# First feed-forward's closing: post steps over two products and the value projection, squares in another order, four adds later

## The chip, the cores and the metric

The kernel runs on one core of a Trainium2 chip. The metric is the device time of one execution in microseconds (us); lower is better. The kernel before takes 2013.42 us, the median of three runs (2012.97 to 2015.08). The engines are named as in the profile: PE (TensorE, matrix products), DVE (VectorE), ACT (ScalarE), POOL (GpSimd) and SP (SyncE, which here issues the transfers).

## The reference

A trunk of two layers over 1024 positions of width 1024, all in float32. Layer A is a gated linear recurrence beside a memory attention; layer B is a sliding-window attention over shared keys and values beside a memory attention. Each is followed by an output projection and a feed-forward of inner width 2816. Around each mixer and each feed-forward stands a norm before and one after ("sandwich"); the one after the feed-forward is the one that the change touches:

```python
def swiglu_ffn(x, w_in, w_out):
    gu = x @ w_in
    g, u = gu[..., :D_FF], gu[..., D_FF:]
    return (jax.nn.silu(g) * u) @ w_out
...
f = swiglu_ffn(rms_norm(h, norm_ffn_pre[l]), w_ffn_in[l], w_ffn_out[l])
h = h + rms_norm(f, norm_ffn_post[l])
if l == N_A_LAYERS - 1:
    kv = rms_norm(h, norm_kv) @ w_kv_shared
```

After the first layer's feed-forward the shared keys (with a partial rotary) and values are projected from the residual; layer B reads them. The last lines of the kernel's feed-forward and the first of layer B therefore follow each other on every engine.

## The kernel before

Every float32 product is made of three matmuls of rounded halves, low by high, high by high and high by low. A tile is split into its halves by a cast on ACT (line 92; the names `th`, `ch`, `ah`, `mkh`) and a subtraction on DVE (line 93; `tl`, `cl`, `al`; `mkl` and `kl` are made by the same pair at 302 and 304). The 1024 positions are two halves of 512, and a tile is 128 x 512.

The feed-forward's output projection is a seven-product scheme. Products 1, 6, 7, 4, 2, 5, 3 run in this order; each has 11 steps of 12 matmuls (L761 to L763) whose operands are loaded and split just in time in rings of a few tiles. Four groups of four accumulators are collected: `c11` and `c21` are the first half of the positions, `c12` and `c22` the second. `c21` is last written behind product 4, `c11` behind product 2. So the first half is whole while products 5 and 3 still run, and its closing lies under these two: `squares` sums the squares of eight tiles (ACT square, DVE addition, L227), PE sums over the partitions with a product by ones (L237), DVE and POOL make the reciprocal root (L241, L242), PE spreads it over the partitions again (L249), and `ffn_post` scales each of the eight tiles (L944), adds the residual that SP has loaded (L947), stores the tile and splits it for the next stage. The second half gets its last addend behind product 3 (L865, and L898, which adds the parts of product 5 to `c22`); its closing is the function `fin`, which layer B calls from `done` in the middle of its value projection.

Layer B's `half` sums the squares of its own norm (`s`, L213), copies the spread root to `rsn` (L253), makes two query products for the memory attention (evicted with `rsn` at L411), two key products with the rotary (`rope`, L1071 to L1074: DVE evicts `kf` and a shuffled copy, POOL multiplies and adds), then four value products (L1183 to L1185, evicted to `vv` by ACT at L349 and DVE at L350), and then six query products with the rotary. Memory keys and values come with two loads (`pb` from `mkv`) and are expanded to `mkh`, `mkl` and `mvv`. PE's products of this stage share three banks named "mm"; a product waits until the one three before it has been evicted. Attention units (scores L382, L383, L1100, L1101 to `ss`, transposes to `tt`, outputs to `oo`) are put between the products by a table of quotas; the products of the later half of the positions serve as their cover.

Every engine takes its instructions in the order of one queue. That order comes from a scheduler that goes by priorities and its own estimates. `self.after(x, y)` binds it without a wait on the chip: x is placed after y in the schedule, no more. `POST_STEPS` lists the steps of products 5 and 3 (`steps[12 * i]`, the first matmul of step i) behind which the eight L944 of the first half are placed. `END_PLACES` does the same for the matmuls that follow L237 and L249. `fin` gives no steps before the change.

Of the kernel before, what the change touches and what calls it, by code (L numbers as in the profile page):

```python
# [10 lines left out]
ALU = mybir.AluOpType  # L11
# [6 lines left out]
KT = D // P  # L18
NM = 256
# [19 lines left out]
NEXT_WEIGHTS = ([("wb", NL), ("wb", NL + 1), ("wk", 0), ("wk", 1), ("wv", 0), ("wv", 1)] +  # L39
                [("wb", j) for j in range(NL)] + [("wo", m) for m in range(KT)])  # L40
OPEN_LEAD = 150
POST_STEPS = 4, 5, 7, 8, 10, 12, 13, 15
LATE_PRODUCTS = 2, 5, 3
OUT_PARTS = {1: (0, 0), 2: (1, 0), 3: (1, 0), 4: (1, 1), 5: (1, 1), 6: (0, 0), 7: (0, 1)}
NO_SYNC = mybir.DependencyInfo(mybir.DependencyClass.NoSync, mybir.DependencyReason.DATA)
# [3 lines left out]
class Trunk:  # L49
# [744 lines left out]
    def ffn(self, layer, x, act, hx, finish, dst, final):  # L794
        nc = self.nc
# [56 lines left out]
        gpost = G_FFN_POST + 8 * layer  # L852
# [19 lines left out]
        def squares(f, tags, who, own):  # L872
            tiles = [(e, self.t(tag)) for e, tag in tags]
            take = self.sums(tiles, who, own)
            for m in range(KT):
                take(m, f[m])
            return [x for _, x in tiles]

        ps, w0 = None, []
        for i, c in ((1, c11), (6, c12), (7, c22), (4, c21)):  # L880
            ps = total(i, [(c, None)], ps)
# [11 lines left out]
        if not final:  # L893
            total(3, [(c12, c12)], ps)
            steps = order[5] + order[3]
            h0 = self.ffn_post(f0, rs, 0, gpost, r0, dst, [steps[12 * i] for i in POST_STEPS])
            for x, y in zip(c22, part):
                nc.vector.tensor_tensor(x, x, y, op=ALU.add)  # L898
            for i, g in zip(END_PLACES, marks):
                self.after(steps[i], g[-1])  # L900

            def fin():
                s = self.t("s")
                for k in range(KT):
                    self.sumsq(s, f1[k], k == 0)
                rs1 = self.rstd(s, "p")[1]
                return self.ffn_post(f1, rs1, 1, gpost, lambda k: self.load(self.part(hx, k, 1), "pb"), dst)

            return (*h0, w0), fin
        self.post(f0, rs, 0, gpost, r0, dst)  # L910
# [226 lines left out]
    def layer_b(self, h0, finish):  # L1137
        nc, a = self.nc, self.a
        mask = self.t("mask", (P, 2 * P))
        nc.sync.dma_start(mask, a["mask"])  # L1140
        y = [[None] * KT for _ in range(2)]
        kk = [[None] * 2 for _ in range(4)]
        vv = [None] * 8
        self.mem_tags = 1

        def half(n, act, f, w0, done):
            acts = [act, act]
            s = self.t("s")
            take = self.sums([(nc.vector, s)], "00000000", ("sq",))
            for k in range(KT):  # L1150
                take(k, f[k])
            rc = self.rcol(s, f"n{n}")
            rs = self.spread(rc, self.t("rsn"))
            tab = []
            for name in ("cos", "sin"):
                t_ = self.t(name)
                nc.sync.dma_start(t_, a[name][:, n * H:n * H + H])
                nc.gpsimd.tensor_tensor(t_, t_, rs, op=ALU.mult)
                tab.append(t_)
            for j in range(2):  # L1160
                w = w0.pop(0) if w0 else self.fetch(("wb", NL + j))
                y[n][NL + j] = self.mem_query(w, acts, n, rs)
                done()
            for j in range(2):
                kf = self.t("kf")
                w = w0.pop(0) if w0 else self.fetch(("wk", j))
                self.rope(kf, self.proj(w, acts, n), tab)
                for e in range(2):
                    gi = 2 * j + e
                    if n == 0:  # L1170
                        kk[gi][n] = self.t(f"kh{gi}", dt=F32R), self.t(f"kl{gi}", dt=F32R)
                    else:
                        kk[gi][n] = self.act_tile()
                    self.kdup(kf, 64 * e, *kk[gi][n])
                done()
            wv = [self.fetch(("wv", j), 4) for j in range(2)]
            for i in range(4):
                ps = self.psum("mm")
                sl = slice(i * P, i * P + P)
                for k in range(KT):  # L1180
                    wh, wl = wv[k // 4]
                    ah, al = act[k]
                    nc.tensor.matmul(ps[:, :NM], al[:, sl], wh[:, k % 4], start=k == 0, stop=False)  # L1183
                    nc.tensor.matmul(ps[:, :NM], ah[:, sl], wh[:, k % 4], start=False, stop=False)
                    nc.tensor.matmul(ps[:, :NM], ah[:, sl], wl[:, k % 4], start=False, stop=k == KT - 1)  # L1185
                if n == 0:
                    v = self.t(f"vv{i}", dt=F32R)
                else:
                    if i % 2 == 0:
                        vt = self.act_tile()  # L1190
                    v = vt[i % 2]
                vv[4 * n + i] = v.rearrange("p (g c) -> p g c", g=4)
                self.vsplit(vv[4 * n + i], ps[:, :NM], rc[:, i:i + 1])
                if i % 2:
                    done()
            for j in range(NL):
                y[n][j] = self.acc_tile()
                self.rope(y[n][j], self.proj(self.fetch(("wb", j)), acts, n), tab)
                done()

        kvf = [self.load(d, "pb").rearrange("p (i c) -> p i c", i=2) for d in self.kv1]
        kv = {}

        def units(n):
            us = []

            def mem(j, e):
                if not kv:
                    kv.update({i: self.mem_expand(kvf, i) for i in range(2)})
                return self.mem_unit(y[n][NL + j], e, kv[j], y[n][NL + j])  # L1210

            for j in range(2):
                for e in range(2):
                    us.append(lambda j=j, e=e: mem(j, e))
            for h in range(2 * NL):
                us.append(lambda h=h: self.swa_unit(h, n, y[n][h // 2], kk, vv, mask))
            return us

        ready = []

        def step(n):
            us, at = units(n), [0]

            def done():
                i = at[0]
                at[0] += 1
                if n == 1 and i == PACED_FROM:
                    self.mms = []
                if n == 0 and i == 9:
                    h1.extend(finish())  # L1230
                if i == 3:
                    for j, u in enumerate(us[:4]):
                        ready.insert(MEM_UNITS[j], u)
                elif i >= 6:
                    ready.extend(us[2 * i - 8:2 * i - 6])
                for _ in range(min(QUOTA[n][i], len(ready))):
                    self.attend(ready.pop(0))

            return done

        h1 = []
        half(0, *h0, step(0))
        half(1, *h1, None, step(1))
        order = [6, 7, 0, 1, 2, 3, 4, 5]
        return self.mix_out(1, y, order, self.h1, ready, [(f"k{h}{i}",) for h in "hl" for i in range(4)])
# [68 lines left out]
```

## Time and profile before

| what | value |
|---|---|
| median of three runs | 2013.42 us |
| the profiled execution | 2016.41 us |
| its span, first to last instruction | 2014.6 us |
| PE / DVE / ACT / POOL busy | 98 / 70 / 51 / 21 % of the span |
| closing of the first feed-forward, products 5 and 3 | about 925 to 990 us |
| layer B up to the value projection's end | 990 to 1031 us |
| attention of layer B, first half | up to about 1215 us |
| second feed-forward's closing | from about 1928 us |

The profiled execution is one of its own and 3.0 us above the median; 1.8 us of it lie outside the span. In a list of instructions the columns are start, duration, engine, line, operation and tiles; the square brackets hold the idle time of the engine just before and what ended it. Several alike in a row are one line (x4), with their common duration. Buffer numbers are left out of the names in the trace and stand in the orders below. A matmul's duration includes its passage through the array; the next one starts earlier than it ends.

### The profile page before, as it was taken

To read this page: it belongs to the slowest core of one execution; us is meant where nothing else is said; L and a number is where in the kernel's file an instruction comes from. 1 tells how busy PE (TensorE), PEld (TensorE's weight loads), DVE (VectorE), ACT (ScalarE), POOL (GpSimd) and SP (SyncE) were. 2 spreads that over 40 slices of the span, in tenths; PEclk is the share of its full clock that TensorE was granted. 3 is DMA by queue.
4 is the path that set the end of the run, shared out by engine and by line. 5 is a ranking of instruction groups with operands and counts; after the bars stand their busy time and mean duration, and the time that the engine had idled before them with its cause. 6 is when DMAs were issued, how large, how long until landed. Compare 5 with 4: busy or idle time off the path is not lost.

```text
span 2014.6 us, 27759 instructions
## 1 busy us (share of the span) xinstructions
PE 1965.2 (98%) x9360; PEld 1633.8 (81%) x9360; DVE 1408.1 (70%) x2345; ACT 1019.3 (51%) x1943; POOL 419.2 (21%) x435
## 2 busy tenths in 40 slices
PE   8999999999999999999999999999999999999997
PEld 7887878888888888888788778887888888888887
DVE  7788867977766676456887888679656655654566
ACT  6678764443444444454534768545333333344551
POOL 0122100034443330000035353100233222300001
PEclk9999999999999999999999999999999999999998
DMA  5422436167668789775454123171644444586653
GB/s 177 160 84 79 152 105 240 68 210 265 227 244 274 251 289 314 236 239 168 148 194 172 65 92 128 58 276 54 204 136 167 158 151 154 194 300 192 218 181 115
DMA packets 182685, 359.60 MB, mean 178 GB/s; under 512 B 20112, under 2 KB 25488, under 8 KB 182544
## 3 DMA queue, kind: packets, MB, share of 16 engines
q1 hardware_dynamic: 182544, 357.85, 52.8%
q8 instruction: 73, 1.20, 0.2%
q14 instruction: 68, 0.56, 0.1%
HBM read 251.86 MB, written 105.91 MB: 178 GB/s over the span
## 4 chain that ended last, share of the span: by engine, by line
PE 80%; DVE 9%; ACT 5%; issue 3%; DMA 2%; POOL 1%; SPq 0%; POOLq 0%; DVEq 0%; ACTq 0%
PE mm L653 13%; PE mm L655 13%; PE mm L654 13%; PE mm L761 6%; PE mm L762 6%; PE mm L763 6%; PE mm L154 5%; PE mm L152 5%; PE mm L153 5%; PE oo L1131 1%; DVE al L93 1%; ACT pb L96 1%; PE oo L237 1%; ACT L96 1%; DVE tl L93 1%
## 5 line engine op out<-in xcount | busy, mean ns | idle before, releaser
L92 ACT CAST ch<-wq 128x512 fp32r<-128x512 f32 x311 | 193.2, 621 | 424.2 <-PE mm L654 217.8
L93 DVE TENSOR_TENSOR cl<-wq,ch 128x512 fp32r<-128x512 f32 x311 | 231.6, 745 | 192.3 <-ACT ch L92 116.2
L653 PE MATMUL mm<-al,ch 128*128 128x512 f32 x640 | 252.4, 394 | 0.0
L655 PE MATMUL mm<-ah,cl 128*128 128x512 f32 x640 | 251.0, 392 | 0.0
L654 PE MATMUL mm<-ah,ch 128*128 128x512 f32 x640 | 250.3, 391 | 0.0
L152 PE MATMUL mm<-al,wh 128*128 128x512 f32 x568 | 228.0, 401 | 9.0 <-DVE al L996 7.4
L154 PE MATMUL mm<-ah,wl 128*128 128x512 f32 x568 | 227.0, 400 | 1.0 <-DVE wl L93 1.0
L153 PE MATMUL mm<-ah,wh 128*128 128x512 f32 x568 | 225.7, 397 | 0.0
L761 PE MATMUL mm<-tl,ch 128*128 128x512 f32 x532 | 207.4, 390 | 2.1 <-DVE tl L93 2.1
L762 PE MATMUL mm<-th,ch 128*128 128x512 f32 x532 | 207.0, 389 | 0.0
L763 PE MATMUL mm<-th,cl 128*128 128x512 f32 x532 | 205.2, 389 | 0.5 <-DVE cl L93 0.5
L653 PE MATMUL mm<-tl,ch 128*128 128x512 f32 x480 | 188.8, 393 | 0.8 <-DVE tl L93 0.8
L655 PE MATMUL mm<-th,cl 128*128 128x512 f32 x480 | 188.4, 393 | 0.0
L654 PE MATMUL mm<-th,ch 128*128 128x512 f32 x480 | 187.3, 390 | 0.0
L664 DVE TENSOR_TENSOR c<-c,mm 128x512 f32<-128x512 f32 x120 | 82.3, 686 | 113.5 <-PE mm L655 113.5
L655 PEld LDWEIGHTS mm<-ah,cl 128*128 128x128 f32 x640 | 120.1, 188 | 28.1
L654 PEld LDWEIGHTS mm<-ah,ch 128*128 128x128 f32 x640 | 120.2, 188 | 26.4
L653 PEld LDWEIGHTS mm<-al,ch 128*128 128x128 f32 x640 | 120.2, 188 | 26.0
L152 PEld LDWEIGHTS mm<-al,wh 128*128 128x128 f32 x568 | 108.5, 191 | 31.6 <-DVE al L996 7.4
L154 PEld LDWEIGHTS mm<-ah,wl 128*128 128x128 f32 x568 | 108.4, 191 | 24.9 <-DVE wl L93 1.7
L153 PEld LDWEIGHTS mm<-ah,wh 128*128 128x128 f32 x568 | 108.4, 191 | 22.8
L761 PEld LDWEIGHTS mm<-tl,ch 128*128 128x128 f32 x532 | 99.9, 188 | 23.6 <-DVE tl L93 1.9
(364 smaller groups left out, 4255.0 us busy)
## 6 DMA issues: line engine op xcount, KB each, us to landing
wq<-in_wi_dram SPq DMA_DIRECT2D x168, 256.0 KB, 4.6
xz<-hd SPq DMA_DIRECT2D x154, 256.0 KB, 4.2
th<-xz SPq DMA_DIRECT2D x154, 256.0 KB, 3.6
wp<-in_wf_dram SPq DMA_DIRECT2D x112, 256.0 KB, 4.2
wz<-wp SPq DMA_DIRECT2D x88, 256.0 KB, 2.4
wq<-wz SPq DMA_DIRECT2D x56, 256.0 KB, 3.6
wraw<-in_wa_dram SPq DMA_DIRECT2D x27, 512.0 KB, 3.4
wq<-in_wf_dram SPq DMA_DIRECT2D x42, 256.0 KB, 3.7
```

What stands on the lines that cost most here:

```text
L92: self.cast = self.nc.scalar.copy(hi, src)
L93: return (eng or self.nc.vector).tensor_tensor(lo, src, hi.bitcast(F32), op=ALU.subtract)
L152: self.mms += [nc.tensor.matmul(out, wh, al, start=i == 0, stop=False), nc.tensor.matmul(out, wh, ah, start=False, stop=False), nc.tensor. ...
L153: nc.tensor.matmul(out, wh, ah, start=False, stop=False),
L154: nc.tensor.matmul(out, wl, ah, start=False, stop=i == len(ks) - 1)]
L653: ins += [mm(out, wh, xl, start=start and k == 0, stop=False, skip_group_check=not start), mm(out, wh, xh, start=False, stop=False, skip_g ...
L654: mm(out, wh, xh, start=False, stop=False, skip_group_check=not start),
L655: mm(out, wl, xh, start=False, stop=k == 3, skip_group_check=not start)]
L664: add = lambda o, x, y: nc.vector.tensor_tensor(o, x, y, op=ALU.add)
L761: ins += [mm(ps[m], wh[:, m], xl[:, cs], start=start and p == 0, stop=False, skip_group_check=not start), mm(ps[m], wh[:, m], xh[:, cs], s ...
L762: mm(ps[m], wh[:, m], xh[:, cs], start=False, stop=False, skip_group_check=not start),
L763: mm(ps[m], wl[:, m], xh[:, cs], start=False, stop=p == NFB // 2 - 1, skip_group_check=not start)]
```

## The change

Four things, all in the order of the work; no operation is added or taken away.

- The eight post steps of the first half are placed behind steps 4, 6, 8, ... 18 of products 5 and 3 (22 steps in all), before behind steps 4 to 15.
- The eight post steps of the second half, before without places, are placed behind the matmuls 6, 18, 30, ... 90 of the 96 of the value projection.
- `squares` begins with the four tiles of `c21` (`f[m - 4]` is the last four, then the first four). Both feed-forwards use it.
- The four adds L898 are placed behind the last matmul of product 3.

```diff
--- before.py
+++ after.py
@@ -39,7 +39,7 @@
 NEXT_WEIGHTS = ([("wb", NL), ("wb", NL + 1), ("wk", 0), ("wk", 1), ("wv", 0), ("wv", 1)] +
                 [("wb", j) for j in range(NL)] + [("wo", m) for m in range(KT)])
 OPEN_LEAD = 150
-POST_STEPS = 4, 5, 7, 8, 10, 12, 13, 15
+POST_STEPS, FIN_STEPS = range(4, 20, 2), range(6, 96, 12)
 LATE_PRODUCTS = 2, 5, 3
 OUT_PARTS = {1: (0, 0), 2: (1, 0), 3: (1, 0), 4: (1, 1), 5: (1, 1), 6: (0, 0), 7: (0, 1)}
 NO_SYNC = mybir.DependencyInfo(mybir.DependencyClass.NoSync, mybir.DependencyReason.DATA)
@@ -873,7 +873,7 @@
             tiles = [(e, self.t(tag)) for e, tag in tags]
             take = self.sums(tiles, who, own)
             for m in range(KT):
-                take(m, f[m])
+                take(m, f[m - 4])
             return [x for _, x in tiles]
 
         ps, w0 = None, []
@@ -895,7 +895,7 @@
             steps = order[5] + order[3]
             h0 = self.ffn_post(f0, rs, 0, gpost, r0, dst, [steps[12 * i] for i in POST_STEPS])
             for x, y in zip(c22, part):
-                nc.vector.tensor_tensor(x, x, y, op=ALU.add)
+                self.after(nc.vector.tensor_tensor(x, x, y, op=ALU.add), steps[-1])
             for i, g in zip(END_PLACES, marks):
                 self.after(steps[i], g[-1])
 
@@ -904,7 +904,8 @@
                 for k in range(KT):
                     self.sumsq(s, f1[k], k == 0)
                 rs1 = self.rstd(s, "p")[1]
-                return self.ffn_post(f1, rs1, 1, gpost, lambda k: self.load(self.part(hx, k, 1), "pb"), dst)
+                return self.ffn_post(f1, rs1, 1, gpost, lambda k: self.load(self.part(hx, k, 1), "pb"), dst,
+                                     [self.vmms[i] for i in FIN_STEPS])
 
             return (*h0, w0), fin
         self.post(f0, rs, 0, gpost, r0, dst)
@@ -1174,15 +1175,17 @@
                     self.kdup(kf, 64 * e, *kk[gi][n])
                 done()
             wv = [self.fetch(("wv", j), 4) for j in range(2)]
+            self.vmms = []
             for i in range(4):
                 ps = self.psum("mm")
                 sl = slice(i * P, i * P + P)
                 for k in range(KT):
                     wh, wl = wv[k // 4]
                     ah, al = act[k]
-                    nc.tensor.matmul(ps[:, :NM], al[:, sl], wh[:, k % 4], start=k == 0, stop=False)
-                    nc.tensor.matmul(ps[:, :NM], ah[:, sl], wh[:, k % 4], start=False, stop=False)
-                    nc.tensor.matmul(ps[:, :NM], ah[:, sl], wl[:, k % 4], start=False, stop=k == KT - 1)
+                    self.vmms += [
+                        nc.tensor.matmul(ps[:, :NM], al[:, sl], wh[:, k % 4], start=k == 0, stop=False),
+                        nc.tensor.matmul(ps[:, :NM], ah[:, sl], wh[:, k % 4], start=False, stop=False),
+                        nc.tensor.matmul(ps[:, :NM], ah[:, sl], wl[:, k % 4], start=False, stop=k == KT - 1)]
                 if n == 0:
                     v = self.t(f"vv{i}", dt=F32R)
                 else:
```

In the changed file the lines from 898 on carry numbers that are 1 higher, from 1177 on 2 or 3 higher: L944 is L945, L947 is L948, L1071 is L1072.

The first place is DVE in the closing of the first feed-forward, ahead of two splits that PE waits for, `tl_1956` and `tl_1968`. The `acc` tiles 7320 to 7323 are `c11`, 7328 to 7331 `c21`, 7324 to 7327 `c22`; `hd` holds the residual. Before, from the row behind `tl_1956`:

```order
L93 TENSOR_TENSOR cl_9083<-wq_9088,ch_9082 128x512
L947 TENSOR_TENSOR acc_7328<-acc_7328,hd_8748 128x512
L93 TENSOR_TENSOR tl_1962_9057<-th_1965_9060,th_1961_9056 128x512
L93 TENSOR_TENSOR cl_9107<-wp_9112,ch_9106 128x512
L898 TENSOR_TENSOR acc_7324<-acc_7324,ah_8756 128x512
L898 TENSOR_TENSOR acc_7325<-acc_7325,al_8757 128x512
L898 TENSOR_TENSOR acc_7326<-acc_7326,ah_8758 128x512
L93 TENSOR_TENSOR al_9304<-acc_7320,ah_9303 128x512
L93 TENSOR_TENSOR al_9311<-acc_7321,ah_9310 128x512
L93 TENSOR_TENSOR al_9318<-acc_7322,ah_9317 128x512
L944 SCALAR_TENSOR_TENSOR acc_7329<-acc_7329,cst,oo_8735 128x512
L93 TENSOR_TENSOR tl_1968_9081<-th_1971_9084,th_1967_9080 128x512
```

Now, from `tl_1956` on:

```order
L93 TENSOR_TENSOR tl_1956_9033<-th_1959_9036,th_1955_9032 128x512
L948 TENSOR_TENSOR acc_7323<-acc_7323,hd_8746 128x512
L93 TENSOR_TENSOR cl_9083<-wq_9088,ch_9082 128x512
L93 TENSOR_TENSOR tl_1962_9057<-th_1965_9060,th_1961_9056 128x512
L93 TENSOR_TENSOR cl_9107<-wp_9112,ch_9106 128x512
L945 SCALAR_TENSOR_TENSOR acc_7328<-acc_7328,cst,oo_8735 128x512
L948 TENSOR_TENSOR acc_7328<-acc_7328,hd_8748 128x512
L93 TENSOR_TENSOR al_9304<-acc_7320,ah_9303 128x512
L93 TENSOR_TENSOR al_9311<-acc_7321,ah_9310 128x512
L93 TENSOR_TENSOR al_9318<-acc_7322,ah_9317 128x512
L93 TENSOR_TENSOR tl_1968_9081<-th_1971_9084,th_1967_9080 128x512
```

Between the two splits stood eleven rows, now nine; three L898 have left, and one L944 with its L947 that stood ahead of `tl_1956` follows behind it.

The second place is DVE at the start of layer B. `s_9907` is the sum of squares of the second half, `mm_9446` the first query product, `pb_9397` the memory keys. Before:

```order
L213 TENSOR_TENSOR s_9907<-s_9907,sq_9921 128x512
L213 TENSOR_TENSOR s_9907<-s_9907,sq_9924 128x512
L411 SCALAR_TENSOR_TENSOR acc_9445<-mm_9446,rsn_9432 128x512
L213 TENSOR_TENSOR s_9907<-s_9907,sq_9927 128x512
L309 TENSOR_TENSOR qs_9844<-acc_9445,qs_9844 64x512
L309 TENSOR_TENSOR qs_10017<-acc_9445,qs_10017 64x512
L304 TENSOR_TENSOR mkl_2102_9815<-pb_9397,mkh_2101_9814 64x256 x4
L304 TENSOR_TENSOR mkl_2105_9830<-pb_9397,mkh_2104_9829 64x256 x2
L411 SCALAR_TENSOR_TENSOR acc_9472<-mm_9473,rsn_9432 128x512
L304 TENSOR_TENSOR mkl_2105_9830<-pb_9397,mkh_2104_9829 64x256 x2
L93 TENSOR_TENSOR mvv_2103_9816<-pb_9399,mvv_2103_9816 128x2x64 x2
```

Now:

```order
L213 TENSOR_TENSOR s_9907<-s_9907,sq_9921 128x512
L213 TENSOR_TENSOR s_9907<-s_9907,sq_9924 128x512
L304 TENSOR_TENSOR mkl_2102_9815<-pb_9397,mkh_2101_9814 64x256 x4
L304 TENSOR_TENSOR mkl_2105_9830<-pb_9397,mkh_2104_9829 64x256 x4
L213 TENSOR_TENSOR s_9907<-s_9907,sq_9927 128x512
L93 TENSOR_TENSOR mvv_2103_9816<-pb_9399,mvv_2103_9816 128x2x64 x2
L93 TENSOR_TENSOR mvv_2106_9831<-pb_9399,mvv_2106_9831 128x2x64 x2
L411 SCALAR_TENSOR_TENSOR acc_9445<-mm_9446,rsn_9432 128x512
L411 SCALAR_TENSOR_TENSOR acc_9472<-mm_9473,rsn_9432 128x512
L309 TENSOR_TENSOR qs_9844<-acc_9445,qs_9844 64x512
```

The two evictions L411 stood ahead of and among the `mkl` rows and now stand behind all of them and behind `mvv`. On ACT the copy `rsn_9432` has moved in the same way behind the eight casts to `mkh` and the four to `mvv`.

The third place is DVE in the value projection. `kf_9542` is the second key product's rotary, `vv_2079` the eviction of the first value product. Before:

```order
L1071 TENSOR_TENSOR kf_9542<-mm_9547,cos_9439 128x512
L1072 STREAM_SHUFFLE r_9572<-mm_9547 128x512
L944 SCALAR_TENSOR_TENSOR acc_7316<-acc_7316,cst,rsp_9938 128x512
L944 SCALAR_TENSOR_TENSOR acc_7317<-acc_7317,cst,rsp_9938 128x512
L944 SCALAR_TENSOR_TENSOR acc_7318<-acc_7318,cst,rsp_9938 128x512
L944 SCALAR_TENSOR_TENSOR acc_7319<-acc_7319,cst,rsp_9938 128x512
L944 SCALAR_TENSOR_TENSOR acc_7324<-acc_7324,cst,rsp_9938 128x512
L944 SCALAR_TENSOR_TENSOR acc_7325<-acc_7325,cst,rsp_9938 128x512
L944 SCALAR_TENSOR_TENSOR acc_7326<-acc_7326,cst,rsp_9938 128x512
L944 SCALAR_TENSOR_TENSOR acc_7327<-acc_7327,cst,rsp_9938 128x512
L350 SCALAR_TENSOR_TENSOR vv_2079_9622<-mm_9597,rcn_2049_9429,vv_2079_9622 128x4x64
L304 TENSOR_TENSOR kl_2071_9578<-kf_9542,kh_2070_9577 64x512 x2
```

Now:

```order
L1072 TENSOR_TENSOR kf_9542<-mm_9547,cos_9439 128x512
L1073 STREAM_SHUFFLE r_9572<-mm_9547 128x512
L945 SCALAR_TENSOR_TENSOR acc_7316<-acc_7316,cst,rsp_9938 128x512
L945 SCALAR_TENSOR_TENSOR acc_7317<-acc_7317,cst,rsp_9938 128x512
L945 SCALAR_TENSOR_TENSOR acc_7318<-acc_7318,cst,rsp_9938 128x512
L945 SCALAR_TENSOR_TENSOR acc_7319<-acc_7319,cst,rsp_9938 128x512
L350 SCALAR_TENSOR_TENSOR vv_2079_9622<-mm_9597,rcn_2049_9429,vv_2079_9622 128x4x64
L945 SCALAR_TENSOR_TENSOR acc_7324<-acc_7324,cst,rsp_9938 128x512
L945 SCALAR_TENSOR_TENSOR acc_7325<-acc_7325,cst,rsp_9938 128x512
L304 TENSOR_TENSOR kl_2071_9578<-kf_9542,kh_2070_9577 64x512 x2
L945 SCALAR_TENSOR_TENSOR acc_7326<-acc_7326,cst,rsp_9938 128x512
L304 TENSOR_TENSOR kl_2073_9584<-kf_9542,kh_2072_9583 64x512 x2
```

Four of the eight L944 have moved behind the eviction `vv_2079`, two of them ahead of the splits `kl`, the others among and behind these. On PE the eight score matmuls of the first memory unit (L382, L383) have moved from ahead of the fourth value product to behind it.

## Rows read from the trace of the kernel before

**Rows 1.** The page's busy times: us, share of the span, instructions.

```profile
PE 1965.2 (98%) x9360; PEld 1633.8 (81%) x9360; DVE 1408.1 (70%) x2345; ACT 1019.3 (51%) x1943; POOL 419.2 (21%) x435
```

**Rows 2.** What PE waited for: us in total, times, longest; the first row is of 820 to 1000 us, the others of 1000 to 1110.

```profile
PE mm L761 <- DVE tl L93: 2.1, 2, 1.5
...
PE ss L382 <- ACT pb L96: 2.7, 2, 1.5
PE mm L1183 <- DVE vv L350: 1.8, 1, 1.8
```

**Rows 3.** DVE in order of time in the closing of the first feed-forward; 957.57 is `tl_1956`, 964.86 `tl_1968`.

```profile
941.75 0.16 DVE L241 TENSOR_SCALAR rcp<-oo 128x4 f32<-128x4 f32 x1 [3.05 <-PE oo L237]
...
948.25 2.72 DVE L944 SCALAR_TENSOR_TENSOR acc<-acc,cst,oo 128x512 f32<-128x512 f32 x4 [2.77 <-PE oo L249]
950.89 0.69 DVE L947 TENSOR_TENSOR acc<-acc,hd 128x512 f32<-128x512 f32 x1
...
957.57 0.68 DVE L93 TENSOR_TENSOR tl<-th,th 128x512 fp32r<-128x512 f32 x1
...
960.58 0.69 DVE L898 TENSOR_TENSOR acc<-acc,ah 128x512 f32<-128x512 f32 x1
...
962.39 1.89 DVE L93 TENSOR_TENSOR al<-acc,ah 128x512 fp32r<-128x512 f32 x3
...
964.86 0.68 DVE L93 TENSOR_TENSOR tl<-th,th 128x512 fp32r<-128x512 f32 x1
```

**Rows 4.** PE in order of time in the same stretch: the two matmuls that waited, and two with 19 starts between them.

```profile
958.40 0.47 PE L761 MATMUL mm<-tl,ch 128*128 128x512 f32 x1 [0.63 <-DVE tl L93]
...
959.18 0.39 PE L761 MATMUL mm<-tl,ch 128*128 128x512 f32 x1
...
963.51 0.39 PE L762 MATMUL mm<-th,ch 128*128 128x512 f32 x1
...
965.59 0.50 PE L761 MATMUL mm<-tl,ch 128*128 128x512 f32 x1 [1.47 <-DVE tl L93]
```

**Rows 5.** The start of layer B in order of time on four engines: SP's issue of the memory keys and values, ACT, DVE, and PE's first matmul of the second key product.

```profile
993.20 1.78 SPq L107 DMA_DIRECT2D pb<-mkv  x2
...
998.11 0.59 ACT L253 COPY rsn<-oo 128x512 f32<-128x512 f32 x1 [0.19 <-PE oo L249]
...
999.45 1.26 ACT L308 CAST qs<-acc 64x512 fp32r<-64x512 f32 x2
1002.21 3.37 ACT L302 CAST mkh<-pb 64x256 fp32r<-64x256 f32 x8 [1.49 <-DMA pb<-mkv]
1005.60 0.90 ACT L92 CAST mvv<-pb 128x128 fp32r<-128x128 f32 x4
...
998.73 0.69 DVE L411 SCALAR_TENSOR_TENSOR acc<-mm,rsn 128x512 f32<-128x512 f32 x1
...
1009.61 0.69 DVE L1071 TENSOR_TENSOR kf<-mm,cos 128x512 f32<-128x512 f32 x1
...
1008.37 0.39 PE L152 MATMUL mm<-al,wh 128*128 128x512 f32 x1
```

**Rows 6.** The value projection: DVE and POOL in order of time, then L944's durations there (shortest, median, longest in ns), then PE's first matmul of the fourth value product and the first of the product behind it.

```profile
1019.12 7.44 DVE L944 SCALAR_TENSOR_TENSOR acc<-acc,cst,rsp 128x512 f32<-128x512 f32 x8
1026.48 0.47 DVE L350 SCALAR_TENSOR_TENSOR vv<-mm,rcn,vv 128x256 fp32r<-128x256 f32 x1
...
1011.13 1.27 POOL L1073 TENSOR_TENSOR r<-r,sin 128x512 f32<-128x512 f32 x1 [9.37 <-DVE r L1072]
...
1019.36 1.65 POOL L1073 TENSOR_TENSOR r<-r,sin 128x512 f32<-128x512 f32 x1 [4.62 <-DVE r L1072]
1021.09 1.61 POOL L1074 TENSOR_TENSOR kf<-kf,r 128x512 f32<-128x512 f32 x1
...
L944 DVE SCALAR_TENSOR_TENSOR acc<-acc,cst,rsp x8: 737/737/1783, 1019.1 to 1025.8; 128x512 f32<-128x512 f32 x8
...
1027.01 0.40 PE L1183 MATMUL mm<-wh,al 128*128 128x256 f32 x1 [1.79 <-DVE vv L350]
...
1031.46 0.39 PE L152 MATMUL mm<-al,wh 128*128 128x512 f32 x1
```

**Rows 7.** Busy time by stretch: the stretch, its length, then busy us and instructions of PE, of its weight loads, of DVE, ACT and POOL, the mean granted clock (1.00 is full), the DMA share and GB/s.

```profile
1012.00:1032.00 20.00, 18.21 (x130) 17.47 (x129) 16.72 (x25) 7.19 (x13) 5.92 (x5) 0.91 0.22 69
1032.00:1075.00 43.00, 40.27 (x191) 33.15 (x190) 37.22 (x56) 21.04 (x53) 22.30 (x23) 1.00 0.84 292
...
1135.00:1155.00 20.00, 15.94 (x87) 12.59 (x86) 16.65 (x50) 14.75 (x42) 5.73 (x13) 0.83 0.00 0
```

**Rows 8.** PE's costliest group in 1075 to 1135 us (line, operation, shape, count, busy us, mean ns, idle before), and one of PE's waits in 1110 to 1215 (us in total, times, longest).

```profile
L152 PE MATMUL mm<-al,wh 128*128 128x512 f32 x41 | 16.3, 399 | 0.0
...
PE oo L1131 <- DVE pl L93: 1.7, 2, 1.5
```

**Rows 9.** The second feed-forward's closing in order of time: PE's three longest waits there, and the split on DVE that is spoken of.

```profile
1962.44 1.19 PE L763 MATMUL mm<-th,cl 128*128 128x512 f32 x4 [0.47 <-DVE cl L93]
...
1967.37 0.62 PE L763 MATMUL mm<-ah,tl 128*128 128x256 f32 x3 [2.34 <-DVE tl L93]
...
1971.64 0.39 PE L761 MATMUL mm<-al,th 128*128 128x256 f32 x1 [0.82 <-DVE acc L865]
...
1971.51 0.68 DVE L93 TENSOR_TENSOR tl<-wp,th 128x512 fp32r<-128x512 f32 x1
```

## The prediction

> **What bounds the kernel now.** I read the page first: TensorE (PE) is busy 98 % of the span [rows 1], so a change that adds no matmul can win only what PE still waits, and lose only by new waits. PE's waits, stretch by stretch, came next [rows 2]: 2.1 us in the closing of the first feed-forward, all for DVE's `tl` (L93); 1.8 us for `vv` (L350) in the value projection; 2.7 us for the exponentials that follow. Then the two engines side by side in those stretches [rows 3 to 6], and last the stretches with a lowered clock [rows 7].
>
> In the closing DVE is late by position, not by load: L241 had idled 3.05 us for PE's L237, and the first L944 2.77 us for PE's L249 [rows 3]; both matmuls stand at a fixed place in PE's queue. From 948.25 on DVE then runs without idle time and hands `tl` to PE 0.63 us late at 958.40 and 1.47 us late at 965.59 [rows 3, 4].
>
> In the value projection eight L944 stand in a row ahead of the first `vv` eviction, 1019.12 to 1026.48 [rows 6]. PE has three "mm" banks there, so its fourth product waits for that eviction until 1027.01. Behind this wait the granted clock falls to its lower level, 1.2 GHz: the mean of 1012 to 1032 is 0.91, which is 18 % of 20 us, 3.6 us, at half speed, 1.8 us lost [rows 7].
>
> **Step 1: the closing of the first feed-forward.** (POST_STEPS, the four adds L898, squares by readiness.) No operation is added; a slot is 0.228 us for a 512-column matmul (19 slots from 959.18 to 963.51 [rows 4]). In the new order L237 stands 6 matmuls earlier in PE's queue and L249 5 earlier, so the L944 chain begins 5 x 0.228 = 1.1 us earlier, at 947.1. Of the chain up to the first late `tl` (948.25 to 957.57, 9.3 us), one L944 (0.66, a quarter of 948.25 to 950.89) and one L947 (0.60, as each L898 from 960.58 to 962.39) move behind it: 947.1 + 9.3 - 1.3 = 955.1, done at 955.8, and PE asks at 958.40 - 0.63 = 957.8. The 0.63 goes. From there to the second late `tl` there were 7.3 us (957.57 to 964.86); three L898 at 0.60 leave, and the rest of the order gives ten operations, 6.1 us: 961.2, done at 961.9, where PE, 0.63 earlier, asks at 963.5. The 1.47 goes too. **Gain 2.1 us**; less, down to 0, only if a DVE input (a weight load or a cast) cannot come 2 us earlier. DVE keeps up in what follows, since the L944 and L947 that are put off go to stretches where PE waited for nothing.
>
> **Step 2: what that sets off at the start of the attention phase.** The four L898 (2.4 us) now stand among the sums of squares there, and the L237 of that sum 21 matmuls later. The order of DVE and ACT therefore puts the expansion of the memory keys (`mkh`, `mkl`) ahead of the copy `rsn` (L253) and of the eviction L411, which before ran at 998.73, before that load had landed [rows 5]. ACT now stands still until `mkv` has landed: 1002.21 before; its issue (993.20) follows the last matmul of product 3 through SP's queue, so I take 1000.1. Behind it: eight casts in 3.4 us (1002.21 to 1005.60), a square at the 0.6 of `rsn`, four `mvv` 0.9, `rsn` 0.6: 1005.6. L411 then frees its bank at 1006.3. PE asks for that bank for the second key product, which ran from 1008.37 and is now due at 1006.3. So nothing, or a few tenths, is lost; bounds 0 (all as computed) and 2.1 (the load lands as late as before). But DVE's first rotary step (L1071, `kf`) was at 1009.61 and stays there: two L411 (0.7 each) and the last of four L309, each behind a cast of 0.63 on ACT, end at 1009.6. The lead of 2.1 us is gone on DVE, though not yet on PE.
>
> **Step 3: the value projection.** (FIN_STEPS.) Four L944 now precede the first `vv`. The eight took 7.36 us, with two of them near 1.78 us instead of 0.74; POOL's L1073 and L1074 ran beside these at 1.65 and 1.61 us, where an L1073 alone took 1.27 [rows 6]. POOL's two end at 1022.7, so the two are in the first half, which stays, and the four cost 2 x 0.66 + 2 x 1.72 = 4.8 us. The row starts 9.5 us after `kf`, at 1019.12 as before; `vv` runs at 1023.9 and ends at 1024.3. PE came to it at 1027.01 - 1.79 = 1025.2; now 2.1 earlier, and 0.9 earlier again because eight score matmuls (L382, L383, half a slot each) stand behind this product in the new order: 1022.2. The wait is 2.1 us and not less than before, and I take it that the clock falls as it did. The product then takes what it took, 1031.46 - 1027.01 = 4.45 us, to 1028.8; the scores 0.9, to 1029.7. The next product also needs the second `vv`, behind three L944, four `kl` (2.8) and itself (0.5): 1024.3 + 5.2 = 1029.5, about even. It began at 1031.46: **PE is 1.7 us ahead there, and so 0.4 of the 2.1 us is given back** (from 2.0 given back, if `kf` is 1.5 late, to 1 us more gained, if the clock stays up).
>
> GPSIMD Engine Reference in the Trainium skill, section Specifications, has GpSimd share its SBUF interfaces with VectorE, contending with DVE instructions that have two SBUF inputs. The long L944 beside L1073 and L1074 agree with that rule, and it speaks against this half of the change: the four L944 left in front of `vv` are the very ones that stand beside POOL's two. Without such contention `vv` would come 2.1 us earlier, PE would not wait, and the lead would be near 4 us.
>
> **Step 4: the rest of the attention phase.** No work is added, but the order of PE changes up to about 1150. In 1032 to 1075 DVE is 87 % busy [rows 7] and the waits for exponentials are bound by DVE: where PE comes earlier it waits longer. Of the 1.7 us of lead I let a quarter go there: **loss 0.4 us** (bounds: none, and all 1.7). In 1135 to 1155 PE is busy 15.9 of 20 us, and the clock mean is 0.83: 6.8 us at half, 3.4 lost [rows 7]. No projection matmul (L152) is among its groups; the 41 in the 60 us before it [rows 8] are its possible cover. In the new order only four projection matmuls move into that stretch, 4 x 0.228 = 0.9 us; I take a **gain of 0.5 us**, bounds: a gain of 0.9 + 3.4 = 4.3 if the clock stays up, a loss of 3 if two waits like the one of 1.5 us there [rows 8] come up anew.
>
> **Step 5: the tail.** `squares` serves the final feed-forward too. There L237 also comes 6 matmuls (1.36 us) earlier, so the waits of 0.47 and 2.34 us [rows 9] shrink to 0 and 1.0. But a `tl` that was split at 1971.51 and was used after the product that waited 0.82 now stands ahead of it in PE's queue, and DVE has two more L584 (0.66, the form of L944) and one more L93 ahead of that `tl`, and one L865 less: 1971.51 - 1.36 + 1.32, done at 1972.15. PE reaches it at 1971.64 - 0.82 - 0.47 - 1.36 = 1969.0, so it waits 3.1 us, and goes on at 1972.15 where it went on at 1971.64: **loss 0.5 us**; bounds a gain of 1.8, if that `tl` comes in time (0.47 + 1.36), and a loss of 2.3, one more wait like the longest here. What follows the last matmul is unchanged.
>
> **Sum** in the profiled execution: -2.1 + 0.4 + 0.4 - 0.5 + 0.5 = -1.3 us, 2016.4 to 2015.1. That execution lies 3.0 us over the median of 2013.4, so I forecast **2012.1 us**. About 0.2 %, 4.0 us, is what a measurement of this kernel can tell from no change.
>
> **Rivals.**
> 1. *The attention stretch fills up.* The lead and the four projection matmuls keep the clock up in 1135 to 1155, and `vv` no longer stops PE: 2.1 + 1 + 4.3 less the tail's 0.5, some 7 us: 2006.5. For it: 5.2 us are lost to the low clock in two short stretches. Against: DVE is 83 % busy in the second (16.65 of 20), and little cover moves in. Chance 0.22.
> 2. *Nothing arrives.* The gain of step 1 is paid back on DVE between 1000 and 1060, because DVE's rotary chain starts at the same time as before: 2013.4. For it: `kf` stays at 1009.6. Against: `vv` needs four L944 less. Chance 0.20.
> 3. *Slower through the `mkv` load.* `rsn`, L411, all L309 and `kf` hang on the landing. With 9.5 us from landing to `kf` and 19.9 from `kf` to the end of the second `vv`, the next product starts at landing + 29.4: 1031.6, as before, if it lands at 1002.2. From there on every us later is a us on the time; at 1005 it makes 2.8, the tail's 0.5 and up to 1.8 for another stretch at half clock: 2018.5. For it: ACT has no other work ahead of the load now, and the same transfer took 9 us from issue [rows 5]. Against: SP's order is nearly the same, so the issue should move with PE. Chance 0.17.
> 4. *The order does not do it*: DVE's inputs hold the closing where it was, 2013.4 plus the tail's 0.5: 2013.9. Chance 0.05.
>
> The forecast's own case has 0.36, with 2009 to 2014. **Range** 2005 to 2018.5: from rival 1 with a little more to rival 3. Faster by over 0.2 %: nearly all of rival 1 and a quarter of the forecast's case, 0.31. Slower by over 0.2 %: most of rival 3 and of the attention stretch's bound of 3, 0.20. Within 0.2 %: 0.49.
>
> **What would show it.** Step 1: PE's waits for `tl` L93 before 990 gone, the last matmul of product 3 some 2 us earlier. Step 2: `rsn` and L411 behind eight `mkh`, L1071 near 1009.6. Step 3: a PE wait of about 2 us for `vv` remains, with two L944 still over 1.7 us. Step 4: the mean clock near 1140 to 1150 still below 0.9. Step 5: a wait of L763 for `tl` near 3 us around 1970. I am wrong if PE still waits in the closing, if L1071 moves by over 1.5 us, or if the attention stretch differs by more than 3 us.

## The result and the profile after

The changed kernel is slower: 2016.91 us, the median of 19 runs, against 2012.97 us of 19 runs of the kernel before beside it; ratio 1.0020 (95 % interval 1.0013 to 1.0027), 3.9 us. A repetition gave 1.0013 (1.0003 to 1.0022). Two executions, one of each kernel, ran in a slower state (2433 and 2783 us) and are in no figure of this document. The profiled execution took 2017.1 us, span 2015.3 us.

What PE waited for, first in 820 to 1000 us, then in 1000 to 1110, to be held against [rows 2]:

```profile
PE mm L761 <- ACT ah L863: 0.3, 1, 0.3
...
PE ss L382 <- ACT pb L96: 3.0, 3, 1.7
PE mm L1186 <- DVE vv L350: 2.0, 1, 2.0
PE mm L152 <- DVE vv L350: 1.3, 1, 1.3
PE oo L249 <- POOL rcp L242: 0.8, 1, 0.8
```

The closing's 2.1 us of waits have shrunk to 0.3. Behind 1000 two waits are new, 1.3 and 0.8 us, and the one for the first `vv` is 2.0 where it was 1.8. The start of layer B and the value projection, to be held against [rows 5, 6] (SP, ACT, POOL, DVE, PE):

```profile
991.08 0.93 SPq L107 DMA_DIRECT2D pb<-mkv  x2
...
1000.09 3.35 ACT L302 CAST mkh<-pb 64x256 fp32r<-64x256 f32 x8 [2.68 <-DMA pb<-mkv]
...
1005.44 1.41 POOL L1159 TENSOR_TENSOR cos<-cos,rsn 128x512 f32<-128x512 f32 x1 [9.22 <-ACT rsn L253]
...
1005.01 1.99 DVE L93 TENSOR_TENSOR mvv<-pb,mvv 128x128 fp32r<-128x128 f32 x4
1006.92 1.28 DVE L411 SCALAR_TENSOR_TENSOR acc<-mm,rsn 128x512 f32<-128x512 f32 x2
1008.29 2.78 DVE L309 TENSOR_TENSOR qs<-acc,qs 64x512 fp32r<-64x512 f32 x4
1011.09 0.69 DVE L1072 TENSOR_TENSOR kf<-mm,cos 128x512 f32<-128x512 f32 x1
...
1020.60 4.79 DVE L945 SCALAR_TENSOR_TENSOR acc<-acc,cst,rsp 128x512 f32<-128x512 f32 x4
1025.32 0.47 DVE L350 SCALAR_TENSOR_TENSOR vv<-mm,rcn,vv 128x256 fp32r<-128x256 f32 x1
...
1030.61 0.48 DVE L350 SCALAR_TENSOR_TENSOR vv<-mm,rcn,vv 128x256 fp32r<-128x256 f32 x1
...
1031.15 0.50 PE L152 MATMUL mm<-al,wh 128*128 128x512 f32 x1 [1.33 <-DVE vv L350]
```

The first L411 ran at 998.73 before, the two run from 1006.92 now; `kf` has gone from 1009.61 to 1011.09, and the product behind the value projection begins at 1031.15, where it began at 1031.46. Products 5 and 3 had brought PE a lead of 2 us; here nothing is left of it. In the kernel before, DVE's four subtractions for `mvv` took less than half as long:

```profile
1007.28 0.90 DVE L93 TENSOR_TENSOR mvv<-pb,mvv 128x128 fp32r<-128x128 f32 x4
```

Starts in different executions are compared below from one matmul, the L653 near 406 us that waits 0.4 us for `tl`: what lies before it is the same in all kernels and shifts by some us from run to run.

| traces | product 3's last matmul begins | product behind the value projection begins |
|---|---|---|
| before, three traces | 584.0 in each | 625.4, 625.5, 624.3 |
| after, four traces | 581.9 to 582.0 | 625.1 to 625.5 |

The tail, to be held against [rows 9], has two waits left in place of three, for `tl` both:

```profile
1966.15 0.90 PE L763 MATMUL mm<-ah,tl 128*128 128x256 f32 x3 [2.30 <-DVE tl L93]
1972.35 0.62 PE L763 MATMUL mm<-ah,tl 128*128 128x256 f32 x3 [1.22 <-DVE tl L93]
```

The granted clock (the stretch, its length, PE's busy us, the mean clock, the DMA share and GB/s; first the kernel before, its first trace, then after), in two stretches of the attention and one of the tail:

```profile
1135.00:1155.00 20.00, 15.94 (x87) 0.83 0.00 0
1200.00:1220.00 20.00, 17.39 (x99) 0.91 0.23 81
1955.00:1975.00 20.00, 16.29 (x111) 1.00 0.58 193
```

```profile
1135.00:1155.00 20.00, 16.24 (x92) 0.83 0.01 3
1200.00:1220.00 20.00, 17.40 (x107) 1.00 0.23 80
1955.00:1975.00 20.00, 16.49 (x104) 0.91 0.68 225
```

Both have stretches at the low level, 1.2 GHz, but not at the same places, and this is not the same in two traces of one kernel either (below). The two profiled executions differ by 0.7 us only (2017.1 and 2016.4): the first trace of the kernel before was a draw with much low clock, some 3 us over its median.

### The profile page after: what moved, and what is told of

It is laid out like the page before. It is cut to its first block, busy times and chain, and to the rows that moved or that the text cites. A ratio compares the mean times of both kernels' runs of the same rounds, so it can differ in the third digit from the quotient of the medians.

```text
span 2015.3 us, 27763 instructions
## 1 busy us (share of the span) xinstructions
PE 1965.1 (98%) x9360; PEld 1633.2 (81%) x9360; DVE 1410.5 (70%) x2345; ACT 1017.6 (50%) x1943; POOL 418.0 (21%) x435
## 4 chain that ended last, share of the span: by engine, by line
PE 81%; DVE 9%; ACT 5%; issue 3%; DMA 2%; SPq 0%; POOL 0%; POOLq 0%; DVEq 0%; ACTq 0%
PE mm L653 13%; PE mm L655 13%; PE mm L654 13%; PE mm L761 7%; PE mm L762 7%; PE mm L763 7%; PE mm L154 5%; PE mm L153 5%; PE mm L152 5%; PE oo L1132 1%; DVE al L93 1%; ACT pb L96 1%; PE oo L237 1%; DVE acc L584 1%; PE tt L1125 1%
## 5 line engine op out<-in xcount | busy, mean ns | idle before, releaser
L93 DVE TENSOR_TENSOR cl<-wq,ch 128x512 fp32r<-128x512 f32 x311 | 236.6, 762 | 187.9 <-ACT ch L92 116.2
L653 PE MATMUL mm<-al,ch 128*128 128x512 f32 x640 | 252.6, 395 | 0.0
L653 PE MATMUL mm<-tl,ch 128*128 128x512 f32 x480 | 189.0, 394 | 0.8 <-DVE tl L93 0.8
L653 PEld LDWEIGHTS mm<-al,ch 128*128 128x128 f32 x640 | 120.4, 188 | 25.9
L673 POOL TENSOR_TENSOR x<-wq,wq 128x512 f32<-128x512 f32 x36 | 50.2, 1394 | 330.5 <-DMA wq<-in_wi_dram 323.0
```

Of the source, the lines that this page charges most:

```text
L93: return (eng or self.nc.vector).tensor_tensor(lo, src, hi.bitcast(F32), op=ALU.subtract)
L653: ins += [mm(out, wh, xl, start=start and k == 0, stop=False, skip_group_check=not start), mm(out, wh, xh, start=False, stop=False, skip_g ...
```

## The experiments

The theories: A, the loss is made behind the wait for the `mkv` load, where `rsn`, L411 and `kf` now stand; B, in the tail; C, by PE's new order in the attention stretch; D, one trace is one draw of where the clock falls; E, the new post steps lose by other rows that they move; F, what is lost is low clock and not waits.

All ratios are to the kernel before, in the same session; intervals in brackets. "Begins" is the product behind the value projection, counted as in the table above; before it is 624.3 to 625.5.

**Once more, before and after.** No edit.

> The kernel before once more, for its clock in every run and a second trace. All theories: ratio 1.000. Theory D (the place where the low clock falls changes from run to run, so that one trace shows one draw): the second trace has other stretches at half clock than the first (which had 1027, 1143 and 1211 us in this part), and the mean clock over its runs lies above the 0.991 that the changed kernel's 19 runs have. If D is wrong, the stretches are the same to within a few us.

> The changed kernel once more. By the clocks of the timed runs so far it loses about 18 us at half clock in a run and the kernel before 14, and what is left is the same, 1998.7 and 1998.8. Theory F (the loss is low clock, not waits): mean clock over these runs 0.9910 to 0.9915 against 0.993 of before, ratio 1.0015 to 1.0025, and a trace with again about 15 us or more of low stretches after 900 us, one near 1966. Theory A alone (the wait behind the load): the same ratio, but clock as before, and 3 to 4 us more of waits in the trace.

Before: 0.9996 (0.9987 to 1.0005), mean clock of 11 runs 0.9929. After: 1.0013, mean clock 0.9916 over 10 runs, and 0.9910 over the 19 before them. With a mean clock c in a time t, t(1 - c) is half of the time that was spent at half speed, and the most that the low clock can have cost; 4 to 5 us of it lie behind the last matmul in every trace, where it costs nothing. It was 14.3 us before (standard error 0.8), 18.2 (0.6) and 16.9 (1.0) after. What is left, t times c, is 1998.8 before and 1998.7 and 1999.3 after. More runs of the kernel before, taken in the same two sessions as these, give 15.1 (0.4; 33 runs) and 14.8 (0.5; 26 runs), with 1998.4 and 1998.7 left. So the work and the waits of the changed kernel add up to about what they were, and 2 to 4 us more of low clock go with its loss of 3 to 4. That they are the whole of the loss is not shown: within the kernel before, over the 33 and the 26 runs, the time rises by only 0.6 to 0.8 us for each us of t(1 - c). The second traces lost 3.4 us at half clock between 900 and 1300 us (before) and 1.7 (after), where the first had 6.8 and 5.1.

**Where the clock falls: three more traces.** No edit.

> The kernel before, one more trace. Theory F: about 3.4 us lost at half clock between 900 and 1300 us and 8.4 from 1900 on, as in its second trace; the 6.8 of its first trace is then the rarer draw. The other: 5 to 7 us in the middle, as often as not.

> The changed kernel, one more trace. Theory F (what the changed kernel loses is low clock): between 900 and 1300 us and from 1900 us on together 12 to 15 us lost at half clock, as in its first trace (15.3). If it is waits, 9 to 12 as in the kernel before (15.1 and 11.8), and 2 us or more of waits on top between 1000 and 1215.

> As look_after1: with the four traces of this kernel then at hand the mean lost at half clock by stretch (before 400 us, 900 to 1300, from 1900 on) is 5, 4 to 5 and 9 by theory F; 5, 3 to 4 and 8.4 by the other.

Lost at half clock from 900 us to the last matmul, all traces: before 9.1, 5.9 and 2.2 us, after 9.3, 3.4, 9.0 and 9.3 (the expectations also count 5 to 7 us behind the last matmul). The means, 5.7 and 7.8, go the way of the timed runs, but within one kernel the traces differ by more than the two means do. The tail's part is plainer: a low stretch begins between 1961 and 1975 us in all nine traces with the new order of the squares there (these four and five of the experiments), in two of the eight with the old; mean loss from 1900 us to the last matmul 2.9 against 2.2 us.

**The new post steps of the first half taken back.**

```diff
-POST_STEPS, FIN_STEPS = range(4, 20, 2), range(6, 96, 12)
+POST_STEPS, FIN_STEPS = (4, 5, 7, 8, 10, 12, 13, 15), range(6, 96, 12)
```

> The changed kernel with the first half's post steps at their old places, nothing else undone. The order then has rsn and L411 ahead of the mkv load again. Theory A (the loss is made where L411 stands behind the load, and kf comes 1.5 us late): kf near 1008 instead of 1011.1, and 2 to 3 us less than the changed kernel: ratio to before 1.0003 to 1.001. Theory C (the new order of PE in the attention stretch loses it): no gain against the changed kernel, ratio 1.0015 to 1.0025.

0.9998 (0.9989 to 1.0007), 2012.46 us. The first L411 is ahead of the load again (996.94), begins: 621.6, and PE's waits between 1000 and 1110 us are these; the one for the first `vv` is gone:

```profile
PE ss L382 <- ACT pb L96: 3.2, 3, 1.6
PE mm L152 <- DVE vv L350: 1.3, 1, 1.3
```

The whole loss goes with this one table of numbers, with the order of FIN_STEPS still in place: for theory A and against C, but not yet against E.

**The second half's steps taken back.**

```diff
-                return self.ffn_post(f1, rs1, 1, gpost, lambda k: self.load(self.part(hx, k, 1), "pb"), dst,
-                                     [self.vmms[i] for i in FIN_STEPS])
+                return self.ffn_post(f1, rs1, 1, gpost, lambda k: self.load(self.part(hx, k, 1), "pb"), dst)
```

> The changed kernel with the second half's post steps without places, all eight ahead of the first vv as before; the order of the attention stretch is then that of before. Theory A: kf stays near 1011, and the wait for vv grows to about 5 us because the eight start 1.5 us later and PE comes 2 us earlier: ratio 1.002 to 1.003. Theory C: the loss goes, ratio 1.000 to 1.0007.

1.0015 (1.0006 to 1.0024), begins: 627.2. PE waits 3.7 us for the first `vv`; the order of the attention stretch is that of before, and the loss stays. Theory C falls. FIN_STEPS helps by 2 us at this place, though no gain in time is measured.

**The load of the memory keys ahead of the weights.** The changed kernel with

```diff
-        kvf = [self.load(d, "pb").rearrange("p (i c) -> p i c", i=2) for d in self.kv1]
+        with self.tc.high_priority(offset=1000):
+            kvf = [self.load(d, "pb").rearrange("p (i c) -> p i c", i=2) for d in self.kv1]
```

> The changed kernel with the load of the memory keys and values issued ahead of the four weight loads of the shared keys and values instead of behind them; the order of the other engines stays but for a few rows. Theory A (everything behind the wait for that load comes late): the eight mkh no longer wait, L411 runs near 1000 instead of 1007, kf near 1006.5 instead of 1011.1, the wait for the first vv goes, and the time falls by 3 to 5 us against the changed kernel: ratio to before 0.9995 to 1.0005, perhaps below. Theory E (the new post steps lose by the other rows that they move, in the attention stretch): ratio 1.0015 to 1.0025 as the changed kernel.

0.9993 (0.9982 to 1.0004), 2012.34 us; begins: 621.3. The casts run at 988 us, and:

```profile
993.45 0.89 DVE L93 TENSOR_TENSOR mvv<-pb,mvv 128x128 fp32r<-128x128 f32 x4
...
1001.81 1.28 DVE L411 SCALAR_TENSOR_TENSOR acc<-mm,rsn 128x512 f32<-128x512 f32 x2
1003.18 3.76 DVE L309 TENSOR_TENSOR qs<-acc,qs 64x512 fp32r<-64x512 f32 x4
1006.95 0.69 DVE L1072 TENSOR_TENSOR kf<-mm,cos 128x512 f32<-128x512 f32 x1
...
1021.19 0.47 DVE L350 SCALAR_TENSOR_TENSOR vv<-mm,rcn,vv 128x256 fp32r<-128x256 f32 x1
```

With all four parts of the change in place and the order of the engines nearly kept, taking away this one wait takes away the loss, 4 us or a little more, and PE comes 4 us earlier to the product behind the value projection. `mvv` costs 0.89 us with POOL idle beside it, 1.99 in the changed kernel; but POOL's scalings now lengthen L309, 3.76 us for four where the changed kernel has 2.78. So the run shows what the wait behind the load costs, and does not take the contention away. Theory E falls, since the other rows stay where the new steps put them. Whether the early load would also gain something in the kernel before was not tried.

**The expansion behind the evictions.** The changed kernel with each cast `mkh` placed behind the second L411, which `self.query` names:

```diff
-            nc.scalar.copy(kh[o:o + 64], kf[r:r + 64])
+            ins = nc.scalar.copy(kh[o:o + 64], kf[r:r + 64])
+            if prev is not None:
+                self.after(ins, prev)
...
-                    kv.update({i: self.mem_expand(kvf, i) for i in range(2)})
+                    kv.update({i: self.mem_expand(kvf, i, self.query) for i in range(2)})
```

> The changed kernel with the casts mkh placed behind the evictions L411, so that rsn and L411 run ahead of the load again, as before the change; post steps at their new places. Theory A: L411 near 998, mkh behind it, kf near 1008 to 1009, 2 to 3 us less than the changed kernel, ratio 1.0000 to 1.001. Theory E: ratio 1.0015 to 1.0025.

0.9997 (0.9988 to 1.0005), begins: 622.2. The expected path was not taken: L411 came to 1002.3 only, because `rsn` still stood behind `mvv` on ACT, and `kf` stayed at 1010.8, since the eight `mkl` now stood ahead of it. What came earlier is the second `vv`, at 1026.77 in place of 1030.61, because the scheduler also put it ahead of the `kl`. So the loss went although L411 and `kf` stayed late: the run speaks for the place, not for the mechanism.

**Parts alone.**

```diff
-POST_STEPS = 4, 5, 7, 8, 10, 12, 13, 15
+POST_STEPS = range(4, 20, 2)
```

> The kernel before with the first half's new post steps alone. Theory A: the order has rsn and L411 behind the load, kf near 1012 and all eight L944 in a row ahead of the first vv, so PE waits some 4 us there instead of 1.8: 3 to 5 us slower, ratio 1.0015 to 1.0025. If the loss needs the other parts of the change: ratio 1.000 to 1.0005.

1.0003 (0.9993 to 1.0013), begins: 627.8. L411 does come behind the load and PE does wait more, 2.7 and 1.7 us in the value projection, but the waits for the exponentials behind it fall from 2.7 to 1.0 us, and no loss is measured. So my expectation was a miss: the new steps cost 4 us only where the other parts are present. Why is not shown; behind the value projection PE's order in this kernel is neither that of before nor that of the changed kernel.

The squares by readiness, first feed-forward, with the adds (`closing`, both edits); then the adds alone (`adds`, the second edit):

```diff
-                take(m, f[m])
+                take(m, f[m if final else m - 4])
...
-                nc.vector.tensor_tensor(x, x, y, op=ALU.add)
+                self.after(nc.vector.tensor_tensor(x, x, y, op=ALU.add), steps[-1])
```

> The kernel before with the squares by readiness in the first feed-forward and the four adds behind product 3, no new post steps, second feed-forward as before. The order from 990 on is that of before but for a few rows. My step 1 says that PE ends product 3 some 2 us earlier. If that lead reaches the end: ratio 0.999. If it only lengthens the wait for the first vv, which hangs on the eight L944 (theory A's chain from kf, which stays bound by the load): ratio 0.9995 to 1.000, and a vv wait of 2 to 4 us.

> The kernel before with the four adds behind product 3 alone. By step 1 the second late tl comes in time because three L898 leave (1.47 us), the first stays 0.63 late: product 3 ends about 1.5 us earlier and the ratio is 0.999 to 0.9995, between 1 and closing's 0.9988. If the gain of closing comes from the squares, 1.000.

`closing` 0.9988 (0.9980 to 0.9997), 2011.57 us: **faster than both kernels**, though the interval ends just under 1. Product 3's last matmul at 581.9, begins: 622.1; the lead of 2 us is there and grows to 3. Over its 11 runs t(1 - c) is 15.0 us as before and t times c 1996.4, some 2 us less: here the gain is in the waits and not in the clock. `adds` 0.9995 (0.9986 to 1.0004), 582.2 and 623.9: the adds bring 1.7 of the 2 us at product 3, and the squares the rest.

`closing` with the second half's steps under the value projection (FIN_STEPS) on top:

```diff
-POST_STEPS = 4, 5, 7, 8, 10, 12, 13, 15
+POST_STEPS, FIN_STEPS = (4, 5, 7, 8, 10, 12, 13, 15), range(6, 96, 12)
...
+                                     [self.vmms[i] for i in FIN_STEPS])
```

> The kernel before with squares by readiness in the first feed-forward, the adds behind product 3 and the second half's post steps under the value projection: the change without the new post steps of the first half and without the new tail. L411 is ahead of the load. If the value projection's part is worth its wait (1.8 us) on top of closing's 0.9988: ratio 0.998 to 0.9985. If the new order of the attention stretch takes that back: 0.9985 to 0.9995. Against not_post (0.9998) it differs in the tail alone: 0.0005 to 0.001 lower if the tail costs a low stretch.

0.9993 (0.9984 to 1.0002), begins: 621.8. The value projection's part adds nothing that can be measured.

**The tail alone, and the change without it.**

```diff
-                take(m, f[m])
+                take(m, f[m - 4 if final else m])
```

> The kernel before with the new order of the squares in the second feed-forward only; everything up to 1900 us is then as before. Theory B (the tail makes much of the loss): the trace of the changed kernel had the tail 0.7 us later, so 0.7 to 2.5 us slower, ratio 1.0003 to 1.0012, with waits of 2.3 and 1.2 us for tl in place of 0.5, 2.3 and 0.8, and the clock lowered near 1966. Theories A and C (the loss is made between 990 and 1215): no more than 0.5 us, ratio 1.000.

> The changed kernel with the old order of the squares in the second feed-forward. All six traces with the new order there have the clock lowered near 1966, none of the four with the old one. Theory B+F (the tail costs a low stretch): 1 to 2 us faster than the changed kernel, ratio 1.001 to 1.0015. If the tail is even, as sq_final alone suggests (1.0006, interval over 1): ratio as the changed kernel's, 1.0015 to 1.0025.

(`not_sq_final` has `f[m if final else m - 4]` in the changed kernel.) 1.0006 (0.9997 to 1.0016) and 1.0012 (1.0002 to 1.0022). Three pairs differ in the tail alone: before and `sq_final` +0.0006, `closing_fin` and `not_post` +0.0005, `not_sq_final` and the changed kernel (1.0013 and 1.0020) +0.0001 to +0.0008. All go one way, but none is clear of its interval: a cost of about 1 us for the tail is likely and not shown.

## Why the prediction was wrong

The forecast was 2012.1 us, 1.3 under the median then known; the kernel came out 3.9 us slower.

- **Step 1 held.** First late `tl` done at 956.02 (forecast 955.8), second at 962.51 (961.9); product 3 ends 2.0 to 2.1 us earlier in all four traces (forecast 2.1). One wait of 0.3 remains, for another operand.
- **Step 2 is the step that failed.** The load landed when forecast (1000.09; 1000.1), `rsn` was done at 1005.4 (1005.6). But the step added up ACT's queue alone, and its 0.9 us for `mvv` are ACT's casts. On DVE the four subtractions for `mvv` stand ahead of L411 too, and they took 1.99 us, where before they took 0.90; the first L411 ended at 1007.6, not 1006.3, and `kf` came at 1011.09, not 1009.6. POOL's scaling of `cos` by `rsn` starts the moment `rsn` is there (1005.44, 1.41 us), and now that is beside `mvv`, two-input work on DVE. It is the contention that I had cited for L944 from GPSIMD Engine Reference of the Trainium skill (Specifications); I did not ask what else it meets when POOL's work moves with `rsn`. The bound for "`kf` 1.5 late" gave 2.0 of the 2.1 given back, and that is what came. Besides, L249 of the second half waits 0.8 us (for POOL's L242, behind the late `kf`): not in the sum. With 2.0 in place of 0.4 given back the prediction's sum comes to 2013.7 us, 1.6 of the 4.8 by which the forecast missed the measured 2016.9. The other 3 lie behind the value projection, where PE begins as in the kernel before.
- **Step 3 held, from `kf` on.** The four L945 took 4.79 (4.8), the wait for the first `vv` 2.0 (2.1), the second `vv` ended 20.0 us after `kf` (19.9). The 1.3 us wait for it is the late `kf`.
- **Step 4 had lost its premise,** the lead, so its loss of 0.4 could not be seen; and its gain of 0.5 did not show. From the product behind the value projection to the first matmul of the second output projection the traces take 744.2, 741.9 and 741.5 us before and 744.4, 742.4, 743.8 and 744.0 after, about 1 us more in the mean; low clock in between (6.8, 3.4 and 0.0 us; 5.1, 1.7, 5.1 and 5.1) and waits are not separated by so few. **Step 5** had the waits in other sizes (2.3 and 1.2 us, forecast 1.0 and 3.1); its loss of 0.5 stands against about 1 us from the three pairs.
- **The low clock was taken as unchanged, and was not.** The waits that were saved and those that came are about equal, 1998.4 to 1998.8 us before and 1998.7 to 1999.3 after without the low clock; t(1 - c) rose from 14 or 15 to 17 or 18 us. Why the same sum of waits goes with more low clock is open: the traces scatter too much to name the stretch, except the tail's 0.7 us. So of the 3.9 us the part that the clock makes is not traced to a cause.
- **Rivals.** The third had the place right, `rsn`, L411 and `kf` behind the `mkv` load, and `mkv_early` shows it; it blamed the landing, which came on time, where the length of the queue behind it was what grew: 11.0 us from landing to `kf`, forecast 9.5. The second is what became of PE's lead: all of it was paid back between 1000 and 1031, with `kf` later and not at its old time; it did not foresee a loss. The first did not come: PE is busy 16.2 of 20 us in 1135 to 1155, before 15.9, and the clock falls there as it did. The fourth did not either: the closing moved as forecast.

## What to carry to other kernels

When order tables are changed, judge each part alone and each taken away: here one part gains 0.12 %, one loses 0.2 % in company and nothing alone, and two do not show. Look at which short operations the new order puts behind a wait for a load: here issuing that load earlier took the loss away. That the early eviction is what counts is not shown, since `post` and `evict_first` have it late without a loss. And when a producer moves, ask which other engine's work starts with it, and beside what that then runs.

## What the runs showed that I had not expected

The granted clock falls at different places in different executions of one kernel: the kernel before had three low stretches between 900 and 1300 us, two, and none in three traces, and lost 6.8, 3.4 and 0.0 us there. Its single executions spread from 2009.2 to 2018.4 us, so one trace is one draw, and a price for a low stretch read from one trace is not what the median pays.
